# Thirty-two more tokens gathered instead of computed densely in the PEER layer of a two-block transformer kernel

## The chip, the cores and the metric

One core of one Trainium2 chip. The metric is the device time of one execution in microseconds (us); lower is better. All data is float32, the inputs lie in DRAM, and one launch computes both blocks.

## The reference, cut to what matters

The kernel computes `second_block(first_block(x, ...), ...)` for 512 tokens of width 1024. The first block is a mixer (neighbourhood attention and HGRN2) with its projections, and then the PEER layer, which is where the change lies:

```python
PEER_HEADS, PEER_NKEYS, PEER_TOPK, PEER_DQ = 8, 128, 16, 256   # 128 * 128 = 16384 experts
def peer_ffn(h, wq, sub_keys, u, v):
    def block(t):                                   # 128 tokens
        q = (t @ wq).reshape(128, 8, 2, 128)
        s = jnp.einsum('tpcd,pckd->tpck', q, sub_keys)
        s1, i1 = lax.top_k(s[:, :, 0], 16)
        s2, i2 = lax.top_k(s[:, :, 1], 16)
        cand = (s1[..., :, None] + s2[..., None, :]).reshape(128, 8, 256)
        cidx = (i1[..., :, None] * 128 + i2[..., None, :]).reshape(128, 8, 256)
        top, pos = lax.top_k(cand, 16)
        idx = jnp.take_along_axis(cidx, pos, axis=-1)
        g = jax.nn.softmax(top, axis=-1)
        a = jax.nn.gelu(jnp.einsum('tpkd,td->tpk', u[idx], t), approximate=False)
        return jnp.einsum('tpk,tpkd->td', g * a, v[idx])
```

Each token thus has 8 × 16 = 128 chosen experts, each a row of `u` and a row of `v`. In `first_block` it stands as `x = x + gt2 * peer_ffn(modulate(rms_norm(x, norm2), sh2, sc2), ...)`; gt2, and the second block's shift, scale and gate, are products of a vector with `w_mod` and `w_ada`.

## The kernel before

**Numbers.** A product is made of three float32r matmuls: each operand is split into a high part (a cast on ScalarE, line 190) and a low part (the difference, on VectorE, line 191), and high × high, high × low and low × high are added up (`proj_T`, `proj_N`, `s_part`, `v_part`; all matmuls are recorded at line 176). Weights come through one ring of four raw buffers `wr` and four each of `wh` and `wl` (pool "weightsM"), 0.524 MB a load, all issued by SyncE (SP).

**Two ways through PEER.** The 512 tokens are four blocks of 128. Blocks 0 to 2, 384 tokens, are dense. For each of 128 blocks of 128 experts, `s_part` (line 683) multiplies the block's rows of `u` with the 384 tokens (24 matmuls of 384 columns into `pS`) and takes Gelu into a tile `S`. 88 of these (`NSP`) are stored in DRAM (`sd`) and read back later as `Sr`, the others are made in the last stretch. The gates of the dense tokens become a matrix `gd` in DRAM, by products of one-hot tables: for a group of 32 tokens, VectorE compares iotas with the chosen indices (`Rh`, `Lq`), `Lq` is multiplied by the gates (24 of 32 tokens on ScalarE, line 879, 8 on VectorE, line 877), one matmul a token adds up the 128 × 128 table into `pG`, ScalarE copies it into `stg`, and 2 MB go to `gd`. There are 12 groups, and the loop's body stands in lines 860 to 887. In the last stretch (from line 922) `W = S * G` is formed for each expert block, split, and `v_part` multiplies it with the block's rows of `v`: 18 matmuls of 512 columns into the six accumulators `po`.

Block 3 is gathered. One of its tokens sits on each partition, and each of its 128 slots is one indirect DMA, issued by GpSimd (POOL, line 839), of one expert's rows of `u` and `v` for every partition: 1.049 MB into a ring `uv` of four. VectorE forms the dot with the token (line 840, into `pscr`), ScalarE takes Gelu, VectorE multiplies the gate and adds the scaled `v` half to `pacc` (line 846). Two slots make a group; `run_gather` says how many groups are to be done by a point of the program: one in each one-hot group, the other 52 in the last stretch.

**Between them: scores and routing.** Eight steps (line 794) load a piece of `wq`, project all tokens, multiply with the keys and copy the scores of each block into four tables `rsc`. After the steps 1, 3, 5 and 7, `gemv_T` (line 247) computes one modulation vector of `w_mod` or `w_ada` through loads into a ring `wg` of two buffers of its own: eight loads of four small matmuls each (`tp`), a row, and column products with `pick`. Then `routing` (line 725) takes a block at a time: 16 top-16 lists (`top16`, line 715) into `sv` and `si`, 64 candidates a head, a second top-16, the positions turned into key numbers by table spreads (`eq`, `sif`), the softmax, and for dense blocks three transposes into `selT`. Beside it run the parts 3 to 51 (`PRE` is 52). The gather's buffers are allocated after the routing's pool is closed (`eR.close()`).

**What sets the order.** Instructions of one engine run in the order that Tile's scheduler lists, which departs from the order of the program where pools and inputs decide. A tile with `bufs=n` is a ring, in which a writer waits until the reader of n uses ago is done; a pool opened after another's close waits for its users; `tc.issue_after(x)` puts a block's instructions behind x. SP issues all loads and stores but the gathers, in one queue.

Of the kernel before, what the change touches and what calls it, by code (L numbers as in the profile page):

```python
# [124 lines left out]
NS = 10  # L125
NSP = 88
PRE = 52
GEN = 3
GR = 1
LAST = 4  # L130
# [5 lines left out]
def program(tc, a, out, tap=None):  # L136
# [37 lines left out]

    def mm(ps, lhs, rhs, first=True, last=True):
        PE.matmul(ps, lhs, rhs, start=first, stop=last)  # L176
# [70 lines left out]
    def gemv_T(pl, ps_pool, wname, part, v, slot, bias, tag="pm"):  # L247
        row = pl.tile([P, D], F32, name="row", bufs=1)
        for h2 in range(2):
            ps = ps_pool.tile([P, 512], F32, name=tag)  # L250
            for h in range(2):
                hf = 2 * h2 + h
                for k0 in (0, 4):
                    w = pl.tile([P, 4, GW], F32, name="wg", bufs=2)
                    DMA.dma_start(w.rearrange("p k n -> p (k n)"), a[wname][4 * part + hf][:, k0 * GW:(k0 + 4) * GW])
                    gemv_rows(ps[:, h * GW:(h + 1) * GW], w, k0)
            S.copy(row[:, h2 * 512:(h2 + 1) * 512], ps)
        ps = ps_pool.tile([P, 512], F32, name=tag)[:, :2 * KT].rearrange("p (k o) -> p k o", o=2)
        for kt in range(KT):
            mm(ps[:, kt, :], row[:, kt * P:(kt + 1) * P], pick[:, v:v + 2])  # L260
        V.tensor_add(modT[:, slot, :], ps[:, :, 0], bias)
# [353 lines left out]
    nd = ND * P  # L615
# [8 lines left out]
    gd = dp.tile([32, P, ND * 4, P], F32, name="gd")  # L624
    sd = dp.tile([NSP, P, ND * P], F32, name="sd")
    mp = pool(eM, "mid")
    gt2T = modT[:, 5, :]
    h2g = {b: mp.tile([P, D], F32, name=f"h2_{b}") for b in range(ND, NB)}
    idx = {b: mp.tile([P, P], I32, name=f"idx{b}") for b in range(ND, NB)}
    gate = {b: mp.tile([P, P], F32, name=f"gate{b}") for b in range(ND, NB)}  # L630
# [3 lines left out]
    def h2_of(b, x):  # L634
        t = h2g[b] if b in h2g else st.tile([P, D], F32, name="h2t")
        r = rstd_of(x, t)
        V.scalar_tensor_tensor(t, x, r, A2, op0=OP.mult, op1=OP.mult)
        V.tensor_add(t, t, B2)
        c0 = b * P
# [58 lines left out]
    for e in range(EARLY):  # L698
        DMA.dma_start(sd[e], s_part(e, V.tensor_tensor))
    eR = ExitStack()  # L700
# [14 lines left out]
    def top16(src, w, val, pos):  # L715
        t = r2.tile([P, P], F32, name="mr", bufs=2)[:, :w]
# [8 lines left out]
    def routing(b, sc):  # L725
        sv = r2.tile([P, 16, 16], F32, name="sv", bufs=2)
        si = r2.tile([P, 16, 16], U32, name="si", bufs=2)
        for j in range(16):
            top16(sc[:, j, :], P, sv[:, j, :], si[:, j, :])
# [39 lines left out]
        for s_ in range(2):  # L769
            eq = r2.tile([P, 8, 16, 16], BF16, name="eq", bufs=2)  # L770
# [496 lines left out]
```

## Time and profile before

| | |
|---|---|
| median of 3 runs | 2346.18 us (2343.89 to 2346.5) |
| the profiled execution, its own time | 2337.86 us |
| its span in the trace | 2336.1 us, 34601 instructions |
| granted clock of TensorE, mean | 0.992 |
| TensorE matmul (PE) busy | 2259.9 us, 97% |
| weight load (PEld) busy | 1942.3 us, 83% |
| VectorE (DVE) busy | 1598.4 us, 68% |
| ScalarE (ACT) busy | 980.3 us, 42% |
| GpSimd (POOL) busy | 249.1 us, 11% |
| moved by DMA | 481.74 MB, mean 206 GB/s |

The span is what the trace covers of the execution. A busy PE is one with a matmul in its pipeline: their ends are modelled and they overlap, so the distance between two starts, not the duration of one, tells the pace. Waits stand in brackets behind a row, with what ended them. The granted clock is the share of 2.4 GHz that TensorE had; the DMA share is the mean of the core's 16 DMA engines.

### The profile page before, as it was taken

Reading aid. Unit: us, or ns where it says so; the run is one execution under the profiler, and the core shown is the slowest. Engines: PE = TensorE matmul, PEld = TensorE weight load, DVE = VectorE, ACT = ScalarE, POOL = GpSimd, SP = SyncE. Lnnn points to the kernel's source line nnn. Section 1 sums busy time; section 2 is a strip of 40 time slices with the busy share of each in tenths; the row PEclk is TensorE's granted clock in tenths of the full one; section 3 lists DMA queues with packets and bytes.
Section 4 is the critical chain, followed back from the end, with each engine's and each line's share of the span. In section 5 each row is a group of like instructions: output and inputs, shape, how many; then the busy total and the mean of one; then the engine's idle time right before and its main releaser. Section 6 shows DMA issues by size and latency. Waiting matters only on the chain. (4 is left out here: it accounts for less than half of the span.)

```text
span 2336.1 us, 34601 instructions
## 1 busy us (share of the span) xinstructions
PE 2259.9 (97%) x13097; PEld 1942.3 (83%) x13097; DVE 1598.4 (68%) x3193; ACT 980.3 (42%) x1828; POOL 249.1 (11%) x159
## 2 busy tenths in 40 slices
PE   7999999998999999999999999999999999989998
PEld 4899986597779999999988888888888786666888
DVE  3674723354359977999689888888898627767344
ACT  4432333333234335877534333333333434446421
POOL 0000000000000000322222222222130000000000
PEclk9999999999999999999999999999999999999999
DMA  7111135625555574999999999999997231120221
GB/s 265 55 57 55 52 118 178 212 101 178 165 196 158 163 258 153 328 320 319 333 360 396 406 347 349 354 362 363 360 380 263 88 103 42 50 86 28 98 92 55
DMA packets 170871, 481.74 MB, mean 206 GB/s; under 512 B 14864, under 2 KB 87952, under 8 KB 153168
## 3 DMA queue, kind: packets, MB, share of 16 engines
q1 hardware_dynamic: 152272, 345.31, 42.7%
q0 software_dynamic: 18432, 134.23, 14.7%
q8 instruction: 103, 1.69, 0.3%
q14 instruction: 64, 0.52, 0.1%
HBM read 431.76 MB, written 46.66 MB: 205 GB/s over the span
## 5 line engine op out<-in xcount | busy, mean ns | idle before, releaser
L191 DVE TENSOR_TENSOR wl<-wr,wh 128x1024 fp32r<-128x1024 f32 (+1 forms) x378 | 456.7, 1211 | 362.3 <-ACT wh L190 359.8
L190 ACT CAST wh<-wr 128x1024 fp32r<-128x1024 f32 (+1 forms) x378 | 394.0, 1043 | 440.4 <-PE pm L176 196.1
L176 PE MATMUL pS<-h2h,wh 128*128 128x384 f32 x1024 | 348.2, 340 | 7.3 <-ACT S L695 7.2
L176 PE MATMUL pS<-h2h,wl 128*128 128x384 f32 x1024 | 346.1, 338 | 0.0
L176 PE MATMUL pS<-h2l,wh 128*128 128x384 f32 x1024 | 345.5, 337 | 0.0
L839 POOL DMA_INDIRECT uv<-in_uv_dram,idx x128 | 225.8, 1764 | 1006.9 <-DVE pacc L846 688.8
L176 PE MATMUL po<-wl,Wh 128*128 128x512 f32 x768 | 299.6, 390 | 1.8 <-DVE wl L191 1.8
L176 PE MATMUL po<-wh,Wl 128*128 128x512 f32 x768 | 299.5, 390 | 0.0
L176 PE MATMUL po<-wh,Wh 128*128 128x512 f32 x768 | 298.9, 389 | 0.0
L176 PEld LDWEIGHTS pS<-h2h,wh 128*128 128x128 f32 x1024 | 193.4, 189 | 11.7 <-ACT S L695 8.7
L176 PEld LDWEIGHTS pS<-h2l,wh 128*128 128x128 f32 x1024 | 193.3, 189 | 2.0 <-issue 0.8
L176 PEld LDWEIGHTS pS<-h2h,wl 128*128 128x128 f32 x1024 | 193.2, 189 | 0.0
L190 ACT CAST Wh<-W 128x384 fp32r<-128x384 f32 x128 | 65.7, 513 | 267.8 <-PE po L176 162.1
L176 PE MATMUL pm<-h2h,wh 128*128 128x512 f32 x432 | 173.5, 402 | 0.2 <-ACT cr L1106 0.2
L176 PE MATMUL pm<-h2h,wl 128*128 128x512 f32 x432 | 171.8, 398 | 0.0
L176 PE MATMUL pm<-h2l,wh 128*128 128x512 f32 x432 | 171.8, 398 | 0.0
L176 PEld LDWEIGHTS po<-wl,Wh 128*128 128x128 f32 x768 | 144.1, 188 | 31.9 <-DVE wl L191 2.6
L176 PEld LDWEIGHTS po<-wh,Wl 128*128 128x128 f32 x768 | 144.1, 188 | 30.3 <-DVE Wl L191 0.3
L176 PEld LDWEIGHTS po<-wh,Wh 128*128 128x128 f32 x768 | 144.2, 188 | 29.2
L846 DVE SCALAR_TENSOR_TENSOR pacc<-uv,dts,pacc 128x1024 f32<-128x1024 f32 x128 | 163.9, 1281 | 1.9
L840 DVE SCALAR_TENSOR_TENSOR pscr<-uv,h 128x1024 f32<-128x1024 f32 x128 | 156.1, 1219 | 1.9 <-DMA uv<-in_uv_dram,idx 0.9
L191 DVE TENSOR_TENSOR Wl<-W,Wh 128x384 fp32r<-128x384 f32 x128 | 70.8, 553 | 47.9 <-ACT Wh L190 47.8
(410 smaller groups left out, 4100.6 us busy)
## 6 DMA issues: line engine op xcount, KB each, us to landing
wr<-in_uT_dram SPq DMA_DIRECT2D x128, 512.0 KB, 6.0
wr<-in_uv_dram SPq DMA_DIRECT2D x128, 512.0 KB, 7.7
gd<-stg SPq DMA_DIRECT2D x12, 2048.0 KB, 12.6
Gt<-gd SPq DMA_DIRECT2D x32, 768.0 KB, 8.4
sd<-S SPq DMA_DIRECT2D x88, 192.0 KB, 3.9
Sr<-sd SPq DMA_DIRECT2D x88, 192.0 KB, 6.8
wr<-in_w_in_dram SPq DMA_DIRECT2D x32, 512.0 KB, 3.6
wg<-in_w_mod_dram SPq DMA_DIRECT2D x32, 512.0 KB, 4.3
```

Of the source, the lines that this page charges most:

```text
L176: PE.matmul(ps, lhs, rhs, start=first, stop=last)
L190: (ehi or S.copy)(hi, src)
L191: (elo or V.tensor_tensor)(lo, src, hi.bitcast(F32), op=OP.subtract)
L839: G.indirect_dma_start(out=uv, out_offset=None, in_=a["uv"], in_offset=bass.IndirectOffsetOnAxis(ap=idx[b][:, j:j + 1], axis=0))
L840: V.scalar_tensor_tensor(scr, uv[:, :D], 1.0, h2g[b], op0=OP.mult, op1=OP.mult, accum_out=dts[b][:, j:j + 1])
L846: V.scalar_tensor_tensor(acc[b], tl[j - j0][:, D:], dts[b][:, j:j + 1], acc[b], op0=OP.mult, op1=OP.add)
```

## The change

Thirty-two tokens, the last of block 2 (`XB`, rows `r0` = 96 to 127), join the gathered ones.

- They have 128 slots each, and four of a token's slots lie side by side: slot g × 32 + j of the 32 tokens is on partitions 32 g to 32 g + 31, so 32 gathers serve them. The tokens' rows of h2, their indices and gates are copied into that shape by DMAs. At the end two matmuls with `pick` add the four partial sums into rows 96 to 127 of the accumulators of block 2.
- The dense part has `nd` = 352 columns: `s_part` multiplies 352, `sd`, `gd`, `S` and `Sr` shrink, one-hot groups are 11. `W` keeps 384 columns, and GpSimd sets the last 32 to zero, so `v_part` is what it was. `NSP` goes from 88 to 84, `PRE` from 52 to 51, and the `S` ring from 10 to 5.
- Gather buffers and accumulators are laid out ahead of the routing pool. Eight groups (`G0`) of block 3 may run once it is routed, one in each one-hot group, 61 in the last stretch. The dot is written over the `u` half of `uv` (no `pscr`).
- The 16 lists of a block are no longer in `routing`: each score step makes its eight lists (four blocks, two halves) behind its modulation product, from a ring of four score tiles. Blocks are routed in the order 3, 0, 1, 2, and the transposes into `selT` stand behind parts 34, 44 and 50 (`HOLD`).
- The modulation products of the score steps load through the ring `wr`, and their copies and column products are made per half.
- All 32 gate multiplications of a one-hot group, and a spread of `sif` (`sfx`), go to ScalarE.

```diff
-NS = 10
-NSP = 88
-PRE = 52
+NS = 5
+NSP = 84
+PRE = 51
+G0 = 8
+G1 = G0 + 11
+BORDER = (3, 0, 1, 2)
+NLIST = 4
+XG = 32
+HOLD = (34, 44, 50)
...
-    def gemv_T(pl, ps_pool, wname, part, v, slot, bias, tag="pm"):
+    def gemv_T(pl, ps_pool, wname, part, v, slot, bias, tag="pm", share=False):
...
-                    w = pl.tile([P, 4, GW], F32, name="wg", bufs=2)
+                    w = wpool["w"].tile([P, 4, GW], F32, name="wr") if share else pl.tile([P, 4, GW], F32, name="wg", bufs=2)
...
+            for k in range(4):
+                mm(ps[:, k, :], row[:, k * P:(k + 1) * P], pick[:, v:v + 2])
+            V.tensor_add(modT[:, slot, 4 * h2:4 * h2 + 4], ps[:, :, 0], bias[:, 4 * h2:4 * h2 + 4])
...
-    nd = ND * P
+    nd = ND * P - XG
...
+        if b == XB:
+            for g in range(XS):
+                DMA.dma_start(h2g[b][g * XG:(g + 1) * XG, :], t[r0:P, :])
...
+            V.scalar_tensor_tensor(uv[:, :D], uv[:, :D], 1.0, h2g[b], op0=OP.mult, op1=OP.mult, accum_out=dts[b][:, j:j + 1])
...
-    def routing(b, sc):
-        sv = r2.tile([P, 16, 16], F32, name="sv", bufs=2)
-        si = r2.tile([P, 16, 16], U32, name="si", bufs=2)
-        for j in range(16):
-            top16(sc[:, j, :], P, sv[:, j, :], si[:, j, :])
+    def routing(b):
+        sv, si = svs[b], sis[b]
...
-            V.tensor_tensor(eq, eq, sif[:, :, s_, :][:, :, :, None].to_broadcast([P, 8, 16, 16]), op=OP.mult)
+            sfx = r2.tile([P, 8, 16, 16], BF16, name="sfx", bufs=1)
+            S.copy(sfx, sif[:, :, s_, :][:, :, :, None].to_broadcast([P, 8, 16, 16]))
+            V.tensor_tensor(eq, eq, sfx, op=OP.mult)
...
-            for j, t in enumerate((sel[0], sel[1], gt_)):
-                PE.transpose(ps[:, j, :], t, ident)
+            with tc.issue_after(after[HOLD[b]].ins):
+                for j, t in enumerate((sel[0], sel[1], gt_)):
+                    PE.transpose(ps[:, j, :], t, ident)
...
-        for i in range(NB):
+        lists = []
+        for i in BORDER:
...
-            S.copy(scs[i][:, 2 * j:2 * j + 2, :].rearrange("p a b -> p (a b)"), ps[:, :GW])
+            sc = r2.tile([P, 2, P], F32, name="rsc", bufs=NLIST)
+            S.copy(sc.rearrange("p a b -> p (a b)"), ps[:, :GW])
+            lists.append((i, sc))
...
+        for i, sc in lists:
+            for m in range(2):
+                top16(sc[:, m, :], P, svs[i][:, 2 * j + m, :], sis[i][:, 2 * j + m, :])
...
-    for b in reversed(range(NB)):
-        routing(b, scs[b])
+    for b in BORDER:
+        routing(b)
+    run_gather(G0)
     eR.close()
...
-            for tg in range(4):
+            for tg in range(min(4, NTG - 4 * b)):
...
-                    if t8 == 24:
-                        V.tensor_tensor(Lh, Lq, bc(g_), op=OP.mult)
-                    else:
-                        for j in range(8):
-                            S.activation(Lh[:, j, :], Lq[:, j, :], AF.Copy, scale=g_[:, tg * 32 + t8 + j:tg * 32 + t8 + j + 1])
+                    for j in range(8):
+                        S.activation(Lh[:, j, :], Lq[:, j, :], AF.Copy, scale=g_[:, tg * 32 + t8 + j:tg * 32 + t8 + j + 1])
...
-            W = d2.tile([P, nd], F32, name="W")
+            W = d2.tile([P, ND * P], F32, name="W")
+            G.memset(W[:, nd:], 0.0)
...
-                run_gather(GR * ND * 4 - (GR * ND * 4 - len(todo)) * (n + 1) // (P - 10))
+                run_gather(G1 + (len(todo) - G1) * (n + 1) // (P - 10))
...
+            if b == XB:
+                for hf in range(2):
+                    mm(po[b, hf][r0:P, :], pick[:, :XG], acc[b][:, hf * 512:(hf + 1) * 512], False, False)
```

How the instructions stand on three engines, before and with the change. A row is a line of that version's code, the operation, the tiles it writes and reads, the shape, and how many alike follow each other.

TensorE at the first modulation product, behind score step 1: `pm<-h2…` are the score projections, `pm<-keysT` the products with the keys, `tp<-wg` or `tp<-wr` the modulation product and `tp<-pick` its columns. Before:

```order
L176 MATMUL pm<-h2l,wh 128x512
L176 MATMUL tp<-wg,cvec 32x256 x4
L176 MATMUL pm<-h2h,wl 128x512
L176 MATMUL pm<-h2h,wh 128x512
L176 MATMUL pm<-h2l,wh 128x512
L176 MATMUL pm<-h2h,wl 128x512
L176 MATMUL pm<-h2h,wh 128x512
L176 MATMUL tp<-wg,cvec 32x256 x4
L176 MATMUL pm<-h2l,wh 128x512
```

With the change:

```order
L184 MATMUL pm<-keysT,pqT 128x128 x3
L184 MATMUL tp<-wr,cvec 32x256
L184 MATMUL pm<-keysT,pqT 128x128 x5
L184 MATMUL tp<-wr,cvec 32x256 x14
L184 MATMUL tp<-pick,row 128x2 x4
L184 MATMUL tp<-wr,cvec 32x256 x16
L184 MATMUL tp<-pick,row 128x2 x4
L184 MATMUL pm<-h2h,wh 128x512
L184 MATMUL pm<-h2l,wh 128x512
```

The products that stood four at a time between projections stand together ahead of the next step. In SP's queue the loads follow suit: eight of `w_mod` or `w_ada`, then four of `wq`, where they alternated before.

VectorE at the lists behind the same kind of step (`sv`, `si` values and places of a list, `wl` the low part of a weight, `modT` the modulation vector). Before, where all lists stand between the parts:

```order
L720 MAX sv<-mr 128x8
L718 MAX_INDEX si<-sv,rsc_4985 128x8
L721 MAX_INDEX si<-sv,mr 128x8
L718 MAX_INDEX si<-sv,rsc_4985 128x8
L191 TENSOR_TENSOR wl<-wr,wh 128x1024 x2
L717 MAX sv<-rsc_4985 128x8 x2
```

With the change, behind an odd score step:

```order
L772 MATCH_REPLACE mr<-sv_5020,rsc 128x128
L773 MAX sv_5020<-mr 128x8
L774 MAX_INDEX si_5024<-sv_5020,mr 128x8
L269 TENSOR_TENSOR modT<-tp,vecs 128x4
L199 TENSOR_TENSOR wl<-wr,wh 128x1024 x4
L770 MAX sv_5021<-rsc 128x8 x2
L771 MAX_INDEX si_5025<-sv_5021,rsc 128x8
L772 MATCH_REPLACE mr<-sv_5021,rsc 128x128
```

Lists now stand among the score steps, and the four splits of the next step's weights have lists ahead of them and behind them, with the sum of the modulation product between.

GpSimd from the routing to the last stretch. Before:

```order
L708 IOTA ior_4976 128x128
L839 DMA uv<-in_uv_dram,idx_4186 128x2048 x128
```

With the change:

```order
L761 IOTA ior_5011 128x128
L736 DMA uv<-in_uv_dram,idx_4196 128x2048 x42
L970 MEMSET W 128x32 x4
L736 DMA uv<-in_uv_dram,idx_4196 128x2048
L970 MEMSET W 128x32
L736 DMA uv<-in_uv_dram,idx_4196 128x2048
```

The memsets of W's last columns stand in the queue of the gathers, one for each expert block.

## Rows read from the trace of the kernel before

**Rows 1.** Stretches: us; busy PE PEld DVE ACT POOL (count); clock, DMA share, GB/s.

```profile
543.00:680.00 137.00, 133.56 (x803) 101.19 (x802) 46.41 (x177) 41.09 (x72) 0.00 (x0) 1.00 0.52 170
680.00:917.00 237.00, 232.36 (x1353) 227.17 (x1351) 203.31 (x841) 91.82 (x128) 5.48 (x4) 0.99 0.59 191
917.00:1186.00 269.00, 263.91 (x1762) 259.52 (x1763) 237.73 (x253) 200.38 (x484) 72.74 (x28) 1.00 0.91 314
1186.00:1765.00 579.00, 577.20 (x2713) 497.95 (x2713) 507.91 (x700) 212.52 (x330) 147.54 (x96) 1.00 0.96 369
1765.00:1840.00 75.00, 75.00 (x333) 62.05 (x332) 55.07 (x79) 27.93 (x41) 1.43 (x2) 1.00 0.52 178
```

**Rows 2.** Timeline of TensorE, neighbouring matmuls: start us, duration us, instruction.

```profile
850.16 0.33 PE L176 MATMUL pS<-h2h,wl 128*128 128x384 f32 x1
850.33 0.33 PE L176 MATMUL pS<-h2h,wh 128*128 128x384 f32 x1
...
1400.68 0.39 PE L176 MATMUL po<-wh,Wl 128*128 128x512 f32 x1
1400.91 0.39 PE L176 MATMUL po<-wh,Wh 128*128 128x512 f32 x1
...
117.81 0.28 PE L176 MATMUL pm<-wl,hTh 128*128 128x256 f32 x1
...
118.89 0.28 PE L176 MATMUL pm<-wl,hTh 128*128 128x256 f32 x1
```

**Rows 3.** Timeline of TensorE, one-hot products (a float32 matmul is two records).

```profile
973.38 3.73 PE L176 MATMUL pG<-Rh,Lq 128*128 128x128 f32 x32
```

**Rows 4.** Timeline of TensorE, a modulation product among the scores.

```profile
578.22 0.64 PE L176 MATMUL tp<-wg,cvec 128*32 128x256 f32 x8 [0.83 <-DMA wg<-in_w_mod_dram]
578.79 0.50 PE L176 MATMUL pm<-h2h,wl 128*128 128x512 f32 x1
...
590.42 1.84 PE L176 MATMUL tp<-pick,row 128*128 128x2 f32 x16
592.12 0.47 PE L176 MATMUL pm<-h2h,wh 128*128 128x512 f32 x1
```

**Rows 5.** The page's costliest groups: busy us, mean ns | idle before, releaser.

```profile
L191 DVE TENSOR_TENSOR wl<-wr,wh 128x1024 fp32r<-128x1024 f32 (+1 forms) x378 | 456.7, 1211 | 362.3 <-ACT wh L190 359.8
L190 ACT CAST wh<-wr 128x1024 fp32r<-128x1024 f32 (+1 forms) x378 | 394.0, 1043 | 440.4 <-PE pm L176 196.1
L176 PE MATMUL pS<-h2h,wh 128*128 128x384 f32 x1024 | 348.2, 340 | 7.3 <-ACT S L695 7.2
...
L176 PEld LDWEIGHTS pS<-h2h,wh 128*128 128x128 f32 x1024 | 193.4, 189 | 11.7 <-ACT S L695 8.7
...
L846 DVE SCALAR_TENSOR_TENSOR pacc<-uv,dts,pacc 128x1024 f32<-128x1024 f32 x128 | 163.9, 1281 | 1.9
L840 DVE SCALAR_TENSOR_TENSOR pscr<-uv,h 128x1024 f32<-128x1024 f32 x128 | 156.1, 1219 | 1.9 <-DMA uv<-in_uv_dram,idx 0.9
```

**Rows 6.** Tile wg from 545 to 690 us.

```profile
DMA to landing us min/median/max: 3.1/4.4/6.3
```

**Rows 7.** Two stretches within the last, columns as in rows 1.

```profile
1226.00:1343.00 117.00, 116.66 (x558) 101.73 (x557) 106.77 (x147) 45.44 (x70) 32.13 (x21) 1.00 1.01 400
1343.00:1693.00 350.00, 350.00 (x1661) 303.80 (x1660) 302.34 (x415) 128.15 (x200) 84.39 (x56) 1.00 0.94 356
```

**Rows 8.** A pause of TensorE and what followed, columns as in rows 1.

```profile
790.00:795.00 5.00, 1.70 (x10) 1.38 (x9) 5.00 (x31) 3.50 (x5) 0.00 (x0) 1.00 0.48 157
...
796.00:799.00 3.00, 3.00 (x11) 3.00 (x11) 3.00 (x13) 0.00 (x0) 0.00 (x0) 0.50 0.24 22
```

**Rows 9.** Timeline of VectorE, one list from its start to the next's.

```profile
814.79 0.07 DVE L718 MATCH_VALUE_LOAD si<-sv,rsc 128x8 f32 x1
...
815.96 0.07 DVE L718 MATCH_VALUE_LOAD si<-sv,rsc 128x8 f32 x1
```

**Rows 10.** Lines of ScalarE from 925 to 1165 us: busy us, mean ns.

```profile
L879 ACT ACTIVATE Lq<-Lq,selT 128x128 f32<-128x128 f32 x267 | 82.2, 392 | 5.1 <-DVE Lq L874 5.1
```

More of the change, by code (lines that the diff above doesn't have):

```diff
@@ L173, in program @@
     DMA.dma_start(vecs, a["vecs"])
+    last_mm = [None]
     def mm(ps, lhs, rhs, first=True, last=True):
-        PE.matmul(ps, lhs, rhs, start=first, stop=last)
+        last_mm[0] = PE.matmul(ps, lhs, rhs, start=first, stop=last)
     class Split:
@@ L699, in program, with gather, run_gather @@
         DMA.dma_start(sd[e], s_part(e, V.tensor_tensor))
+    ug = pool(eM, "uvg", 1)
+    nfB = ug.tile([P, D], F32, name="nfB")
+    DMA.dma_start(nfB, a["rows"][0:1, :].to_broadcast([P, D]))
+    S.activation(nfB, nfB, AF.Square)
+    gt2 = ug.tile([P, D], F32, name="gt2")
+    acc = {b: ug.tile([P, D], F32, name=f"pacc{b}") for b in range(ND, NB)}
+    eU = ExitStack()
+    up = pool(eU, "uv", 4)
+    ux = pool(eU, "uvx", 1)
+    acc[XB] = ux.tile([P, D], F32, name="paccx")
+    dts = {b: ux.tile([P, n], F32, name=f"dts{b}") for b, n in ncol.items()}
+    for b in acc:
+        V.memset(acc[b], 0.0)
+    GRP = 2
+    def gather(b, j0):
+        tl = []
+        for j in range(j0, j0 + GRP):
+            uv = up.tile([P, 2 * D], F32, name="uv")
+            G.indirect_dma_start(out=uv, out_offset=None, in_=a["uv"], in_offset=bass.IndirectOffsetOnAxis(ap=idx[b][:, j:j + 1], axis=0))
+            V.scalar_tensor_tensor(uv[:, :D], uv[:, :D], 1.0, h2g[b], op0=OP.mult, op1=OP.mult, accum_out=dts[b][:, j:j + 1])
+            tl.append(uv)
+        ds_ = dts[b][:, j0:j0 + GRP]
+        S.activation(ds_, ds_, AF.Gelu)
+        V.tensor_mul(ds_, ds_, gate[b][:, j0:j0 + GRP])
+        for j in range(j0, j0 + GRP):
+            V.scalar_tensor_tensor(acc[b], tl[j - j0][:, D:], dts[b][:, j:j + 1], acc[b], op0=OP.mult, op1=OP.add)
+    todo = [(b, j0) for b, n in ncol.items() for j0 in range(0, n, GRP)]
+    prog = [0]
+    def run_gather(upto):
+        for k in range(prog[0], min(upto, len(todo))):
+            gather(*todo[k])
+        prog[0] = max(prog[0], upto)
     eR = ExitStack()
@@ L783, in routing @@
         V.reciprocal(ts_, ts_)
-        gt_ = gate[b] if b in gate else r2.tile([P, P], F32, name="gt_")
+        gt_ = gate[b] if b >= ND else r2.tile([P, P], F32, name="gt_", bufs=2)
         V.tensor_tensor(gt_.rearrange("p (h k) -> p h k", k=16), tm, ts_[:, :, None].to_broadcast([P, 8, 16]), op=OP.mult)
-        if b in idx:
+        if b == XB:
+            xf = r2.tile([P, P], F32, name="xf")
+            xi = r2.tile([P, P], I32, name="xi")
+            V.scalar_tensor_tensor(xf[r0:P], sel[0][r0:P], 128.0, sel[1][r0:P], op0=OP.mult, op1=OP.add)
+            V.tensor_copy(xi[r0:P], xf[r0:P])
+            for g in range(XS):
+                DMA.dma_start(idx[b][g * XG:(g + 1) * XG, :], xi[r0:P, g * XG:(g + 1) * XG])
+                DMA.dma_start(gate[b][g * XG:(g + 1) * XG, :], gt_[r0:P, g * XG:(g + 1) * XG])
+        if b >= ND:
             V.scalar_tensor_tensor(sel[0], sel[0], 128.0, sel[1], op0=OP.mult, op1=OP.add)
@@ L848, in program @@
-    todo = [(b, j0) for b in range(ND, NB) for j0 in range(0, P, GRP)]
-    prog = [0]
-    def run_gather(upto):
-        for k in range(prog[0], min(upto, len(todo))):
-            gather(*todo[k])
-        prog[0] = max(prog[0], upto)
     with ExitStack() as es:
```

78 lines of the change are left out of this document (30 added, 48 removed).

## The prediction

> **What bounds the kernel now.** I read the stretches first [rows 1]: they are cut at the first score projection (543 us), the last score (680), the first one-hot product (917), the first product with V (1186), the last gather (1765) and the last product with V (1840). TensorE is busy 97 to 100% of every one, so it sets the end. A busy TensorE need not be at its pace, so next the start-to-start distances [rows 2]: 173 ns for 384 columns, 227 for 512, 120 for 256 (1.08 us for nine). That is 0.418 ns a column plus 13 ns, at 2.4 GHz (the granted clock is 0.99 to 1.00). One expert block's U product ("part": 24 matmuls of 384 columns) therefore takes 4.15 us, one block's V product (18 of 512) 4.09 us. Against these sums, how much of a stretch is lost? 543 to 680: eight score steps of 48 × 0.227 + 16 × 0.114 = 12.7 us [rows 2, 3] and four modulation products of 8 × 0.57 + 1.70 = 6.3 us [rows 4] make 127 of 137 us. 680 to 917: 55 parts, 228 of 237. 917 to 1186: 41.5 parts and 768 one-hot records of 0.114 us make 260 of 269. 1186 to 1840: 28.5 parts, 128 V blocks and the gt2 spread make 644 of 654. So nearly all is matmul time, and only fewer columns, or fewer stalls, shorten it. What may stop such a saving is in the DMA column [rows 1]: 0.91 and 0.96 of 16 engines busy in the third and fourth stretch.
>
> **The change part by part.**
>
> *Narrower U products.* 128 × 24 = 3072 matmuls (a third of them are the 1024 of [rows 5]) go from 384 to 352 columns: 32 × 0.418 = 13.4 ns each, **-41.1 us**, all on the engine that bounds. The V products keep 512 columns and their number.
>
> *One group of one-hots fewer.* 32 matmuls, 64 records at 0.114 us [rows 3]: **-7.3 us**.
>
> *Modulation products out of the weight ring.* Before, they had their own two buffers and stood between score matmuls. Now their eight loads use the four buffers of the weights, and the order shows them in a clump. I follow one clump from t = 0, the end of an odd step's scores. The first four loads are in: products until 2.2. Their buffers' next loads leave at 0.6, 1.2, 1.7 and 2.3. The first lands a median 4.4 us later [rows 6], the others behind it at about 1.3 us (0.524 MB at the 400 GB/s of rows 7): 5.0 to 8.9, the last product ends at 9.5, and copy and column products at 11. Behind them in SP's queue stand the next step's weights, which need the fifth and sixth buffer: issued at 5.6, landed at about 10.2, cast by 11.3 (1.04 us), split by VectorE (1.2 us) [rows 5] at 12.5. Only then can TensorE's third matmul run. So 12.5 us where 6.3 are work: 6.2 of stall, four times, 25 us; less the 10 lost there now, and 1 to 2 us because the first split behind the last clump stands behind routing instructions: **+16 us**. Queued behind the wait: on TensorE all scores, on VectorE the four splits (behind the modulation's add). Bounds: 0 (the loads run ahead as now) to +28 (each landing the slowest, 6.3 us).
>
> *The clock.* TensorE did 1.7 us of work in 790 to 795, and then had 0.50, which is 1.2 GHz, in 796 to 799 [rows 8]. A clump does some 4 us of work in the 10 us from 2.2 on, so I expect a dip at each. Three us at half pace behind the restart cost 1.5: **+6 us**, bounds 0 and +14.
>
> *Lists behind the scores.* 64 lists at 1.17 us [rows 9]. Eight of them take 9.4 us: those of an even step run under the 12.7 us of the next, those of an odd one are done before the weights above are split. Cost 0; if the clump got shorter than 9.4 us, they would be what is late next. Taking 75 us of VectorE work out of 680 to 917 (203 busy of 237) makes room for 16 gathers (2.35 us each beside the others) and should halve the 9 us lost there: **-4 us**, bounds -9 and +5.
>
> *Gates on ScalarE, one-hot stretch.* The 32 gate multiplications of a group, 24 now, cost 0.31 us each [rows 10]: 2.5 us more on ScalarE, 1.2 less on VectorE. A group then holds 18.8 us of TensorE (3 × 3.84 + 64 × 0.114), some 19 of ScalarE (200 busy in 269 now, which is 15 of 20 for a group with all its copies, less overlap, plus 2.5: 17.5 to 19.3), and 6.3 MB, 18.3 us at 314/0.91 = 345 GB/s. Three engines level lose more to each other than one bound: **+4 us** over 11 groups, bounds 0 and +15. The two table spreads a block (ScalarE copies) run where ScalarE is busy 92 of 237 us: 0.
>
> *The last stretch.* Nine parts move into it (39 instead of 30). To the last gather it has 118 V blocks (482 us) and 36 parts of 3.84 (138): 620 us of TensorE. In that time it moves 118 V blocks and 36 U blocks at 0.524 MB, 122 gathers at 1.049 (61 groups; now 104), 77 S of 0.18, 29.5 G of 0.72: 244 MB, which is 393 GB/s, where 369 are moved now at 0.96 busy. VectorE: 508 of 579 now; 26 gathers and 8 splits more make some 580 of 620, not the bound. DMA is level with TensorE. For 117 us it did 400 GB/s with TensorE 99.7% busy [rows 7], so I take **+10 us**; bounds 0 and +41 (the mean rate of the stretch). The Trainium skill speaks against it: "DMA: Bandwidth & Descriptors", Specifications, gives an HBM limit of about 358 GB/s a core and a derate of 368. By the latter 244 MB would take 663 us, 43 more than TensorE's; rows 7 exceed it for 117 us, so I don't take it for the sum.
>
> *POOL.* The memsets of W's last 32 columns queue behind gathers that wait for a buffer. No row has such a wait: 0 where the casts' lead of several VectorE instructions covers it, at most a gather's issue (147.54 us for 96 in the fourth stretch [rows 1], 1.5 each) in an iteration; inside the bounds above. The 32-row copies of h2, indices and gates: SP has time; 0. The correction's two matmuls, and the second row copy of the three earlier modulation products: **+1 us**.
>
> Sum: -41.1 - 7.3 + 16 + 6 - 4 + 4 + 10 + 1 = **-15 us**. The profiled execution took 2337.9 us, 8.3 below the median 2346.2; I take the difference from the median: **2331 us**. A measurement of this kernel tells about 0.2%, 4.7 us.
>
> **Rivals.**
>
> *DMA becomes the bound of the last stretch: slower.* Place: 1186 to the last gather. If the engines give no more than the stretch's mean of 369 GB/s, it lasts 661 us: +41 where I have +10, sum +16, 2362 us. The gain is gone below 244/(620 + 25) = 378 GB/s. For it: 0.96 busy, and 356 GB/s at 0.94 over 350 us [rows 7], though TensorE lost nothing there. Against: the 400 GB/s. By the 368 of the Trainium skill's section above it would come to 2364. Chance 0.20.
>
> *The clumps cost nothing.* If loads lead as they do now, the 16 and 6 go and the sum is -37: 2309 us. For it: SP's queue is nearly empty there (0.52 busy). Against: the ring has four buffers, and a clump needs ten. Chance 0.15.
>
> *Clumps dearer, one-hot stretch level.* +28 and +14 in place of 16 and 6, and +10 at the groups: 2357 at the worst, about 2346 at half of it, no change. Chance 0.14.
>
> *The columns save nothing.* A weight load shows 189 ns [rows 5], longer than the 173 between starts, and loads are busy all through. If they set the pace, the 41 us are lost: 2372. Against: 256 columns, with the same loads, start every 120 ns. Chance 0.04.
>
> **How the numbers follow.** The forecast has 0.47, nearly all of it faster. Faster: 0.44 + 0.15 + a little of the third rival = 0.60; same: 0.15, from the third rival and the forecast's edge; slower: 0.20 + 0.04 + 0.01 = 0.25. Range 2304 to 2362: it holds the forecast with the bounds of single terms, the second rival, the third, and the first up to its own price; the loads' case and a DMA worse than that lie outside. The forecast's own range is 2315 to 2342.
>
> **What would show it.** U matmuls 160 ns apart; four idle stretches of 4 to 8 us between 550 and 700 whose releaser is a load of wr, dips of the clock at them, and the first routing part 15 to 20 us later than 680; groups of 19 to 19.5 us; first V product at about 1125 to 1135; the stretch from there to the last V product 690 to 700 us with DMA at 0.98. Wrong: loads of wr or uv as the main releasers of TensorE or VectorE in that stretch (first rival), or no idle time at the clumps (second).

## The result and the profile after

The change takes 2367.04 us (median of 6 runs, 2365.09 to 2372.22) where the kernel before takes 2346.34 (6 runs): ratio 1.0094, 95% interval 1.0076 to 1.0113. It is 20.7 us slower. The prediction said 2331 and a range up to 2362, so both the time and the sign were missed.

The profiled execution took 2367.62 us. The page's first lines:

```profile
span 2365.8 us, 34863 instructions
...
PE 2250.0 (95%) x13037; PEld 1915.8 (81%) x13037; DVE 1644.6 (70%) x3295; ACT 1001.0 (42%) x1908; POOL 314.1 (13%) x319
```

The stretches, cut at the same events, with the columns of [rows 1]:

```profile
547.00:695.00 148.00, 134.69 (x734) 101.32 (x733) 88.86 (x470) 34.53 (x65) 0.00 (x0) 0.88 0.37 129
695.00:931.00 236.00, 217.33 (x1342) 209.63 (x1340) 195.00 (x607) 107.81 (x150) 31.12 (x20) 0.96 0.74 267
931.00:1160.00 229.00, 216.70 (x1518) 212.77 (x1517) 190.00 (x199) 196.07 (x515) 45.70 (x24) 0.98 0.91 312
1160.00:1795.00 635.00, 619.59 (x2935) 530.41 (x2935) 564.11 (x792) 224.88 (x360) 211.09 (x233) 0.99 0.96 374
1795.00:1866.00 71.00, 70.90 (x329) 58.73 (x327) 54.53 (x80) 27.98 (x41) 4.41 (x14) 1.00 0.50 178
```

TensorE's work did shrink. Two neighbouring U products on its timeline start 160 ns apart, where [rows 2] has 173:

```profile
781.19 0.32 PE L184 MATMUL pS<-h2h,wh 128*128 128x352 f32 x1
781.35 0.32 PE L184 MATMUL pS<-h2l,wh 128*128 128x352 f32 x1
```

So a part costs 3.84 us for 4.15, as forecast, and with the one-hot group the matmuls need some 47 us less. Everything else is time that TensorE now loses. For each stretch I compare its length with what its matmuls need at their own pace (parts, V blocks of 4.09 us, one-hot records of 0.114 us). "Scores" runs from the first copy of the projected queries to the last product with the keys, "routing" from there to the first copy of a one-hot product, "last" from the first to the last product with V; what stands between is the one-hot stretch:

| stretch, us | before | needs | lost | change | needs | lost |
|---|---|---|---|---|---|---|
| ahead of the scores | 553.3 | | | 547.5 | | |
| scores | 127.1 | | | 147.6 | | |
| routing | 238.5 | 229 | 9 | 235.6 | 206 | 30 |
| one-hot groups, first S tiles | 267.4 | 258 | 10 | 228.9 | 211 | 18 |
| last | 653.7 | 653 | 1 | 706.3 | 679 | 27 |
| behind | 496.0 | | | 500.0 | | |

The scores grew by 20.5 us with the same matmuls but for 16 small ones that now stand in the routing, and the routing, the one-hot stretch and the last one lose 55 us more than before. By the records in the trace these three need 44 us less. With 5.8 us less ahead and 3.9 more behind, that is 29.6 us; the two executions differ by 29.8. The medians differ by less, because the execution profiled of the kernel before lay 8 us under its median. I therefore take the size of a cause from timed runs, and its place from the traces.

### The profile page after: what moved, and what is told of

It reads as the page before. It is cut to its first block, busy times and chain, and to the rows that moved or that the text cites. A ratio compares the mean times of both kernels' runs of the same rounds, so it can differ in the third digit from the quotient of the medians.

```text
span 2365.8 us, 34863 instructions
## 1 busy us (share of the span) xinstructions
PE 2250.0 (95%) x13037; PEld 1915.8 (81%) x13037; DVE 1644.6 (70%) x3295; ACT 1001.0 (42%) x1908; POOL 314.1 (13%) x319
## 5 line engine op out<-in xcount | busy, mean ns | idle before, releaser
L736 POOL DMA_INDIRECT uv<-in_uv_dram,idx x160 | 274.2, 1714 | 841.9 <-DVE pacc L743 501.6
L184 PE MATMUL pS<-h2h,wh 128*128 128x352 f32 x1024 | 338.8, 331 | 13.0 <-ACT S L712 13.0
L184 PE MATMUL pS<-h2h,wl 128*128 128x352 f32 x1024 | 336.8, 329 | 3.9 <-DVE wl L199 3.7
L184 PE MATMUL pS<-h2l,wh 128*128 128x352 f32 x1024 | 335.6, 328 | 0.0
L737 DVE SCALAR_TENSOR_TENSOR uv<-uv,h 128x1024 f32<-128x1024 f32 x160 | 192.7, 1219 | 24.2 <-DMA uv<-in_uv_dram,idx 23.8
L740 ACT ACTIVATE dts<-dts 128x2 f32<-128x2 f32 x80 | 16.3, 204 | 259.4 <-DVE uv L737 259.4
L913 ACT ACTIVATE Lq<-Lq,selT 128x128 f32<-128x128 f32 x352 | 109.4, 394 | 4.6 <-DVE Lq L911 4.6
```

The lines of the kernel that those rows point to most:

```text
L184: last_mm[0] = PE.matmul(ps, lhs, rhs, start=first, stop=last)
L736: G.indirect_dma_start(out=uv, out_offset=None, in_=a["uv"], in_offset=bass.IndirectOffsetOnAxis(ap=idx[b][:, j:j + 1], axis=0))
L737: V.scalar_tensor_tensor(uv[:, :D], uv[:, :D], 1.0, h2g[b], op0=OP.mult, op1=OP.mult, accum_out=dts[b][:, j:j + 1])
L740: S.activation(ds_, ds_, AF.Gelu)
L913: S.activation(Lh[:, j, :], Lq[:, j, :], AF.Copy, scale=g_[:, tg * 32 + t8 + j:tg * 32 + t8 + j + 1])
```

## The experiments

Lengths of stretches are cut as in the table above, ratios are to the kernel before. Four of the results side by side, the others in the text:

| run | median us | ratio | interval |
|---|---|---|---|
| own_buffers | 2340.51 | 0.9987 | 0.9972 to 1.0002 |
| no_extra_gathers | 2342.56 | 0.9997 | 0.9983 to 1.0011 |
| odd_half_rows | 2339.09 | 0.9984 | 0.9963 to 1.0005 |
| own_spread_ten | 2318.20 | 0.9882 | 0.9854 to 0.9910 |

### own_buffers: the modulation products out of the shared ring

```diff
-                    w = wpool["w"].tile([P, 4, GW], F32, name="wr") if share else ...
+                    w = up.tile([P, 2 * D], F32, name="uv")[:, :4 * GW].rearrange("p (k n) -> p k n", n=GW) if share else ...
```

> The change, but the modulation products of the score steps load into the four gather buffers, which are idle then, and not into the ring of the weights. In the change the scores take 147.6 us from the first projection to the last product with the keys (before: 127.1), with four clumps of modulation products, pauses of some 5 us and 10 to 14 us at half clock at each. Theory A, the shared ring is the cause: the scores go back to 125 to 132 us, the four low-clock stretches between 570 and 720 us go, and the time falls by 20 to 30 us, to 2337 to 2347. Rival, the lists or the score tiles (a ring of four) hold the scores back: the stretch stays above 140 us and the time at 2360 or more.

The ratio falls from 1.0094 to 0.9987, some 25 us. The scores take 125.9 us and the routing 229.6, 21.7 and 6.0 less (the fourth clump stands at the routing's start). Theory A holds. In the change, TensorE's timeline at the first clump reads:

```profile
571.40 1.05 PE L184 MATMUL tp<-pick,row 128*128 128x2 f32 x8 [0.69 <-ACT row L265]
573.38 0.64 PE L184 MATMUL tp<-wr,cvec 128*32 128x256 f32 x8 [0.93 <-DVE sv L773]
574.57 0.64 PE L184 MATMUL tp<-wr,cvec 128*32 128x256 f32 x8 [0.55 <-DMA wr<-in_w_mod_dram]
576.85 1.08 PE L184 MATMUL tp<-wr,cvec 128*32 128x256 f32 x8 [1.64 <-DMA wr<-in_w_mod_dram]
578.10 1.08 PE L184 MATMUL tp<-wr,cvec 128*32 128x256 f32 x8 [0.17 <-DMA wr<-in_w_mod_dram]
579.94 1.86 PE L184 MATMUL tp<-pick,row 128*128 128x2 f32 x8 [0.76 <-ACT row L265]
581.67 0.77 PE L184 MATMUL pm<-h2h,wh 128*128 128x512 f32 x1
582.24 0.63 PE L184 MATMUL pm<-h2l,wh 128*128 128x512 f32 x1
582.67 0.63 PE L184 MATMUL pm<-h2h,wh 128*128 128x512 f32 x1
```

The pauses in brackets add up to 4.7 us, most of them for a load of `wr` or for the row's copy. The clock adds to them: behind the clump 512 columns are 0.43 us apart, not 0.227. The stretches around it, columns as in [rows 1]:

```profile
565.00:576.00 11.00, 8.04 (x76) 5.13 (x75) 7.75 (x52) 2.47 (x6) 0.00 (x0) 0.98 0.48 166
576.00:586.00 10.00, 8.22 (x35) 5.51 (x36) 7.51 (x23) 4.57 (x5) 0.00 (x0) 0.51 0.80 278
586.00:596.00 10.00, 10.00 (x48) 7.96 (x46) 0.85 (x1) 1.17 (x2) 0.00 (x0) 1.00 0.51 170
```

The granted clock is 1.2 GHz for 10 us. It is so at each of the four clumps, for 10.2, 10.2, 13.7 and 13.7 us; [rows 8] had shown about 3. Part of these times TensorE stands idle, so by estimate (half of the rest) each costs 4 to 6 us: the four clumps lose 20 us in pauses and some 18 by the clock, about as much. In own_buffers no low clock falls inside the scores, whose row reads:

```profile
554.00:680.00 126.00, 122.68 (x755) 92.86 (x754) 93.36 (x474) 38.57 (x69) 0.00 (x0) 1.00 0.56 182
```

VectorE does the lists there as in the change (93 us of work), at no cost.

### before_shared_ring: that part alone

```diff
-        gemv_T(rb, tp, "w_mod", 5, 0, 5, bmT[:, 40:48], "tp")
+        gemv_T(rb, tp, "w_mod", 5, 0, 5, bmT[:, 40:48], "tp", True)
...
-            gemv_T(rb, tp, "w_ada", part, 2, 6 + part, baT[:, part * 8:part * 8 + 8], "tp")
+            gemv_T(rb, tp, "w_ada", part, 2, 6 + part, baT[:, part * 8:part * 8 + 8], "tp", True)
```

> The kernel before with one part of the change alone: the modulation products of the score steps load into the ring of the weights. Theory, the shared ring makes the clumps: the scores go from 127 us to 140 to 150, low-clock stretches of 10 us and more show at the modulation products, and the time rises by 18 to 28 us, ratio 1.008 to 1.012. Rival, it needs the lists behind the scores too (they delay the column products' add on VectorE): under 10 us.

Ratio 1.0162 (1.0116 to 1.0208): 38 us, even more than forecast. The scores take 154.6 us and the routing 253.3, together 42 more than before, and the clock is at half for 13.7 us at each of the first three products. The row of the scores, which had 1.00 in the clock's column before:

```profile
571.00:726.00 155.00, 138.29 (x743) 104.35 (x745) 38.27 (x173) 35.04 (x66) 0.00 (x0) 0.87 0.36 123
```

The lists aren't needed for it. Its profiled execution shows 18 us more ahead of the scores as well, where the edit changes nothing that I can name. TensorE is at half clock there for 51 us in its trace and for 17 in that of the kernel before, and half of the difference is 17 us, which by estimate is the 18; why the clock was low more often stays open.

### no_extra_gathers: the price of the 32 gathers

```diff
-    todo = [(b, j0) for b, n in ncol.items() for j0 in range(0, n, GRP)]
+    todo = [(b, j0) for b, n in ncol.items() if b != XB for j0 in range(0, n, GRP)]
```

> The change without its 32 extra gathers (the 32 tokens get no PEER output; the routing, copies and narrower products stay). In the change the stretch from the first to the last product with V is 706 us for 676 us of matmuls, DMA 0.97 busy at 374 GB/s. Theory A, the last stretch is bound by DMA with the extra 33.6 MB (90 us at 374 GB/s, of which TensorE's own work covers most): it falls to 676 to 684 us and the time by 20 to 30 us, to 2337 to 2347. Rival, the narrower stages lose their time for other reasons (GpSimd's memsets, the shorter S ring): it stays above 695 us, and the time at 2355 or more.

The ratio falls to 0.9997, 23 us, and the last stretch from 706.3 to 681.0 us, with 679 needed. Its row up to the last gather shows a TensorE that never waits:

```profile
1156.00:1743.00 587.00, 586.50 (x2832) 508.60 (x2832) 486.40 (x669) 216.66 (x336) 148.41 (x196) 1.00 0.91 342
```

So the two causes, clumps and extra gathers, are worth 25 and 23 us. Together they are what the columns and the one-hot group saved; that they add up wasn't tried in one run. The change is 21 us slower all the same, so some 20 us more are lost elsewhere, by the table in the routing and the one-hot stretch.

### What in the gathers costs: half_bytes, odd_half_rows, odd_no_sum, zero_once

The waits of the last stretch (engine, what waits, for what; us, times, longest) name more than one engine. Before:

```profile
POOL uv L839 <- DVE pacc L846: 415.5, 63, 17.3
ACT Wh L190 <- PE po L176: 157.9, 67, 3.3
ACT dts L843 <- DVE pscr L840: 65.2, 26, 7.0
...
ACT wh L190 <- DMA wr<-in_uv_dram: 11.8, 9, 3.5
```

The change:

```profile
POOL uv L736 <- DVE pacc L743: 214.2, 64, 8.4
ACT dts L740 <- DVE uv L737: 212.1, 55, 9.3
POOL W L970 <- DVE Wl L199: 112.4, 47, 9.4
ACT wh L198 <- DMA wr<-in_uv_dram: 87.6, 43, 7.2
```

ScalarE, which used to wait for TensorE, now waits for loads of V and for the dots. In both kernels GpSimd waits for VectorE's sum before it can issue the next gather, since the sum frees the buffer. Four runs separate bytes, VectorE and GpSimd.

half_bytes fetches half rows for the 32 extra gathers:

```diff
-            G.indirect_dma_start(out=uv, out_offset=None, in_=a["uv"], ...
+            G.indirect_dma_start(out=uv if b != XB else uv[:, :D], out_offset=None, in_=a["uv"] if b != XB else a["uv"].rearrange("n (t d) -> (n t) d", d=D), ...
...
```

> The change with the 32 extra gathers fetching half a row, 4 KB a partition in place of 8, and the sum taken from that half (the 32 tokens' PEER output is not the reference's). GpSimd issues as many gathers, VectorE and ScalarE do the same work on them; only 16.8 MB of transfers go. Theory DMA: what the extra gathers cost in the last stretch (706 us against 681 without them) is their bytes; at 374 GB/s half of them are 45 us of the DMA engines, more than the 25 lost, so the stretch falls to 680 to 690 us and the time by 15 to 25 us, to 2342 to 2352. Rival, engines' order (ScalarE behind the dots, VectorE 0.89 busy, GpSimd's longer queue): the stretch stays above 700 and the time at 2360 or more.

Ratio 1.0090 (1.0067 to 1.0114), last stretch 701.8 us: by the letter the rival's numbers. But the edit was badly placed. The extra gathers are the last in the list, so only the last quarter moved fewer bytes. Its windows (columns as in [rows 1]) show the loss ahead of that point and none behind it:

```profile
1170.00:1570.00 400.00, 384.39 (x1828) 326.74 (x1828) 351.71 (x499) 138.58 (x224) 135.77 (x147) 1.00 0.96 370
...
1650.00:1791.00 141.00, 141.00 (x680) 122.06 (x679) 134.19 (x188) 54.20 (x86) 47.71 (x55) 1.00 0.87 297
```

odd_half_rows therefore does it to every second gather of the whole list:

```diff
+            half = j % 2 == 1
-            G.indirect_dma_start(out=uv, out_offset=None, in_=a["uv"], ...
+            G.indirect_dma_start(out=uv[:, :D] if half else uv, out_offset=None, in_=a["uv"].rearrange("n (t d) -> (n t) d", d=D) if half else a["uv"], ...
...
```

> The change with every second gather (80 of 160, over the whole last stretch, not the last quarter alone as in half_bytes) fetching half a row, and the sum taken from that half (wrong output). The count of gathers and the work of every engine stay; 42 MB of transfers go, some 32 MB of them in the last stretch. Theory DMA: the last stretch, 706 us for 679 of matmuls, falls to 679 to 684 us, and the time by 22 to 35 us, to 2332 to 2345. Rival, VectorE and ScalarE waiting on each other in order: it stays above 697 us and the time above 2355.

The last stretch takes 679.0 us, its matmuls' own time, with VectorE as busy as in the change:

```profile
1162.00:1762.00 600.00, 600.00 (x2898) 521.14 (x2899) 563.27 (x792) 224.95 (x359) 218.97 (x232) 1.00 0.94 345
```

odd_no_sum keeps the bytes and leaves out every second weighted sum:

```diff
-        for j in range(j0, j0 + GRP):
+        for j in range(j0, j0 + GRP, 2):
             V.scalar_tensor_tensor(acc[b], tl[j - j0][:, D:], ...
```

> The change with the weighted sum left out for every second gathered slot (wrong output): 80 VectorE instructions of 1.28 us fewer, 61 of them (78 us) in the last stretch, and their buffers come free after the dot. The bytes stay. Theory DMA: the last stretch stays at 695 to 708 us. Rival, VectorE (0.89 busy there) or the return of the buffers holds the stretch: it falls to 679 to 688 us. The routing has 8 such sums fewer: 4 to 8 us less in either case. Time 2350 to 2362 by the first, 2330 to 2345 by the second.

The ratio is 1.0062 (1.0035 to 1.0089). The last stretch, 688.2 us, lies in neither theory's range, nearer the rival's; the time, 2356.92, lies in the first one's. So neither is right alone. Its row is the surprise:

```profile
1165.00:1771.00 606.00, 599.78 (x2882) 518.78 (x2883) 498.91 (x730) 223.50 (x359) 160.89 (x231) 0.99 0.99 390
```

The same transfers went through at 390 GB/s. So 374 isn't all that the DMA engines give. My reading is that with four buffers, each held until VectorE has formed its sum, they are not asked for more; no run has more buffers, and the edit takes work from VectorE as well as freeing buffers sooner, so these two aren't told apart. The pace that the change needs is 374 × 635 us over the 608 that remain without the loss, 390 GB/s. I read the two runs together so: that pace is out of reach while the buffers return late, and nearly within reach when they don't. Fewer bytes recover all of the 27 us, fewer sums two thirds. (The routing took 237.4 us; the 4 to 8 us that I expected there didn't come.)

zero_once takes the memsets out of GpSimd's queue:

```diff
+        Ws = [d2.tile([P, ND * P], F32, name=f"W{i}", bufs=1) for i in range(2)]
+        for W in Ws:
+            G.memset(W[:, nd:], 0.0)
...
-            W = d2.tile([P, ND * P], F32, name="W")
-            G.memset(W[:, nd:], 0.0)
+            W = Ws[n % 2]
```

> The change with two fixed W tiles whose last 32 columns GpSimd sets to zero once, in place of a memset for each expert block. In the change GpSimd's memsets waited 150 us in the last stretch for a free W, with gathers queued behind them. Theory DMA: the memsets cost nothing, since a gather that leaves later finds the DMA engines just as full: the last stretch stays at 700 to 710 us and the time within 4 us of the change's, 2363 to 2371. Rival, the memsets hold the gathers back: the stretch falls to 690 or less and the time by 10 us or more.

Ratio 1.0114 (1.0085 to 1.0142), last stretch 701.5 us. GpSimd's 112 us of waiting for W cost nothing that can be told.

### Where the gathers stand: own_early, own_late, own_spread

Every run whose name begins with own_ has the edit of own_buffers too, which the diffs don't repeat; own_early also has both table spreads on VectorE.

```diff
-NSP = 84
-PRE = 51
+NSP = 96
+PRE = 63
...
-G0 = 8
+G0 = 22
...
```

> The change with four edits: the modulation products load into the idle gather buffers; both table spreads stay on VectorE; 12 U products of the last stretch stand in the routing (63 ahead of the one-hot groups, 96 stored); 22 groups of gathers in place of 8 are issued ahead of the one-hot groups. The columns saved are the same. The last stretch then moves by estimate 216 to 224 MB in 628 us of TensorE's work, 345 to 357 GB/s, under the 374 at which it lost time. Theory DMA and clumps: the last stretch loses under 8 us against its matmuls (it takes 628 to 640 us), the scores take 126, and the time falls below before's, to 2312 to 2328, ratio 0.986 to 0.994. Rival, the routing stretch has no room for 14 more groups on VectorE or ScalarE (2.4 us a gather on an engine that is 0.82 busy): TensorE loses 20 to 35 us more there, and the time is 2335 to 2350.

2360.68 us, ratio 1.0085 (1.0059 to 1.0112): the rival's way, and over its range by 11 us. The last stretch is freed, 634.4 us for 633 of matmuls at 364 GB/s, but the routing takes 310.1 us for 257, and the one-hot stretch loses 19 us more than in own_buffers. That the added parts and gathers only move the loss is what the run shows; its four edits aren't separated.

```diff
-G0 = 8
+G0 = 0
```

> The change with the modulation products in the gather buffers and no group of gathers ahead of the one-hot groups (0 for 8): 16 gathers, 16.8 MB, move into the last stretch. Beside own_buffers (routing 230 us, last stretch 708, 2340 us). Theory DMA: at 374 GB/s they add 45 us to a stretch that is full, so it takes 745 to 755 us, the routing gives back 5 to 12 us (its early gathers hold ScalarE and VectorE), and the time is 2370 to 2385. Rival, the last stretch isn't bound by bytes: it grows by under 15 us, and the time stays at 2335 to 2352.

2388.45 us, ratio 1.0199 (1.0178 to 1.0219), a little over the range. The last stretch takes 759.8 us, 52 more than in own_buffers for 16 gathers, 3.2 us each. Its row up to the last gather:

```profile
1116.00:1804.00 688.00, 638.23 (x2937) 536.30 (x2938) 599.51 (x849) 226.02 (x368) 252.61 (x248) 0.97 0.96 369
```

With more bytes to move, the engines moved them no faster than in the change, and below the 390 of odd_no_sum. The routing, with no gather's arithmetic in it, takes 213.1 us and loses 7. Taken together, own_late, own_buffers and own_early make a line: 0, 16 and 44 early gathers lose 7, 24 and 53 us in the routing, some 1.05 us for each. own_early has other edits there too, so this is no more than an indication.

own_spread moves nothing between stretches, it only lets the gathers of the last one run on for six blocks more:

```diff
-                run_gather(G1 + (len(todo) - G1) * (n + 1) // (P - 10))
+                run_gather(G1 + (len(todo) - G1) * (n + 1) // (P - 4))
```

> The change with the modulation products in the gather buffers, and the gathers of the last stretch spread over 124 expert blocks in place of 118. In the change the DMA engines are 0.97 busy until the last gather and 0.50 busy in the 70 us behind it. Theory DMA: a pace 5% lower, 370 MB/ms on the mean of the whole stretch, is near what they move (374), so most of the loss goes: last stretch 685 to 697 us where own_buffers has 708, time 2322 to 2334. Rival: the late sums now stand ahead of the last products and uncover 5 to 10 us at the end, or the loss isn't the pace: 2338 to 2348.

2328.15 us, ratio 0.9930 (0.9903 to 0.9956). The last stretch falls from 708.1 to 693.7 us: the DMA engines were half idle behind the last gather (0.50 in the change's last row above), and that time is now used.

### Smaller parts: ten_s_tiles, gates_spread_back, own_spread_ten

```diff
...
+    s5 = pool(eU, "sbuf5", 5)
+    ring = lambda e: sbuf if (e - NSP) % 10 < 5 else s5
-    for _ in range(NS):
+    for _ in range(10):
         e = fresh.pop(0)
-        Ss[e] = s_part(e)
+        Ss[e] = s_part(e, None, ring(e))
...
```

> The change with ten S tiles ahead of the last stretch in place of five (five more in the space that the one-hot stage leaves). Theory: the five parts fewer uncover the trip of the last group through DRAM (7.0 us of pause at 1152 us, behind it 6.8 us at half clock): the pause falls to under 3 us and the time by 5 to 9 us, to 2358 to 2362. Rival: the parts are only moved, the DMA of the last stretch sets its end, which comes no sooner with 5 loads less in it or the pause covered: 2364 to 2369. If S tiles also give the last stretch more lead: 2350.

2360.83 us, ratio 1.0080 (1.0050 to 1.0110). The median fits, the interval takes in the change's own ratio. The trace shows one pause of 2.6 us there in place of the 7.0 us ahead of the first V product.

```diff
-            sfx = r2.tile([P, 8, 16, 16], BF16, name="sfx", bufs=1)
-            S.copy(sfx, sif[:, :, s_, :][:, :, :, None].to_broadcast([P, 8, 16, 16]))
-            V.tensor_tensor(eq, eq, sfx, op=OP.mult)
+            V.tensor_tensor(eq, eq, sif[:, :, s_, :][:, :, :, None].to_broadcast([P, 8, 16, 16]), op=OP.mult)
...
-                    for j in range(8):
+                    if t8 == 24:
+                        V.tensor_tensor(Lh, Lq, bc(g_), op=OP.mult)
+                    for j in range(8 if t8 < 24 else 0):
```

> The change with a quarter of the gate multiplications and both table spreads back on VectorE, as before. In the change the one-hot groups lose 8 us more against their matmuls than before, and ScalarE waits 15 us for the spreads in the routing, with TensorE behind it. Theory A, ScalarE is the wrong place: the time falls by 6 to 14 us, to 2353 to 2361. Rival, VectorE is as full there (191 busy of 230 us): 2365 to 2375.

Ratio 1.0109 (1.0078 to 1.0139): no gain, the rival. Routing and one-hot stretch are 3.0 and 3.6 us shorter in its trace, too little to show in the times.

own_spread_ten is own_spread with the ten S tiles and the spreads on VectorE:

> own_spread, with both table spreads back on VectorE and ten S tiles ahead of the last stretch. Theory: ten S tiles cover the trip of the last one-hot group (4 to 8 us) and the spreads no longer hold ScalarE in the routing (3 us): 2312 to 2326, ratio 0.987 to 0.993, the fastest so far. Rival: these are within the noise of own_spread: the same time within 4 us.

Its ratio of 0.9882 is 28 us under the kernel before, the fastest of all; its interval lies under own_spread's median. The last stretch:

```profile
1156.00:1784.00 628.00, 628.00 (x2955) 531.86 (x2954) 565.15 (x788) 229.81 (x363) 195.30 (x233) 1.00 0.98 377
1784.00:1829.00 45.00, 45.00 (x191) 34.80 (x189) 39.55 (x61) 17.06 (x25) 6.04 (x8) 1.00 0.50 179
```

TensorE has no pause up to the end. With the loads (own_buffers), the pace (own_spread) and the cover of the last group (ten S tiles) put right, 28 of the some 47 us saved are kept.

### The early gathers: own_early_no_gelu, own_early_dma_only

ScalarE's timeline in own_buffers shows how a gather in the routing may hold TensorE. ScalarE runs in order, the Gelu of a part stands behind these, and TensorE's next part behind that Gelu:

```profile
800.32 0.20 ACT L740 ACTIVATE dts<-dts 128x2 f32<-128x2 f32 x1 [4.75 <-DVE uv L737]
...
838.26 1.90 ACT L826 COPY sfx<-sif 128x2048 bf16<-128x2048 bf16 x1 [7.74 <-DVE eq L827]
```

```diff
+        if prog[0] >= G0:
             S.activation(ds_, ds_, AF.Gelu)
```

> The change with the modulation products in the gather buffers, and the Gelu of the eight early groups left out (wrong output): ScalarE no longer stands waiting for the dots of those groups, VectorE and the transfers do the same. own_buffers' routing took 229.6 us, own_late's (no early group) 213.1. Theory A, ScalarE's order holds TensorE (it waited 20 us for the dots and 24 for the spreads' tables there): the routing falls to 215 to 222 us. Rival, VectorE is simply full while it routes: 226 to 231 us.

The routing takes 224.3 us, between both ranges: 5.3 of the 16.5 us over own_late. The time is 2333.55, ratio 0.9955 (0.9931 to 0.9978). But own_spread, whose code differs from own_buffers' in the last stretch alone, has a routing of 225.7 us in its trace, so two traces of one routing differ by 3.9. The 5.3 are hardly more than that, and the intervals of this ratio and of own_buffers' overlap.

```diff
+            if prog[0] < G0:
+                continue
             V.scalar_tensor_tensor(uv[:, :D], uv[:, :D], 1.0, h2g[b], ...
...
+        if prog[0] < G0:
+            return
         ds_ = dts[b][:, j0:j0 + GRP]
```

> As own_early_no_gelu, with the dots and sums of the eight early groups left out too (wrong output): the 16 gathers are only transfers. Theory A or VectorE: 212 to 216 us, as without early groups. Rival, the transfers delay the loads of U's rows: 222 us or more.

233.1 us (time 2345.53, ratio 0.9991, 0.9968 to 1.0014): the transfers alone cost as much as the whole gathers. The run took the pace away with the work, though. Nothing held the buffers, the gathers went off back to back, and loads of U came late. Of ScalarE's waits in the routing the row on them reads:

```profile
ACT wh L198 <- DMA wr<-in_uT_dram: 34.2, 9, 7.5
```

The window of the burst, columns as in [rows 1]:

```profile
760.00:800.00 40.00, 30.33 (x155) 28.88 (x153) 27.56 (x118) 15.01 (x17) 10.64 (x9) 0.87 1.02 421
```

own_buffers has no such wait among its large ones. So the early gathers cost 13 to 17 us in the routing (own_late against own_spread and own_buffers). ScalarE's order is not shown to be a large part of it, and how the loss divides between that, VectorE, the spreads' tables and the transfers stays open.

## Why the prediction was wrong

**Right.** The columns and the one-hot group saved what was said. The clumps were forecast at 22 us (16 and 6), and own_buffers takes out 25 in time, 27.7 in the stretches. ScalarE's gates and the memsets cost little or nothing.

**The clock term.** Its sum hid two errors that cancel in part. The pauses are shorter than worked out, 20 us over the four clumps for 25; the half clock is longer. I took three us behind a restart from [rows 8], 1.5 us lost each, 6 in all. It lasted 10 to 14 us, some 18 lost in all. (own_buffers keeps about 8 us of both at these places, so about 30 of the 38 go with its edit; its stretches show 27.7.) What [rows 8] shows is a single pause with full work behind it; a clump is a series of pauses among small matmuls. Which of these makes the difference wasn't tried.

**The last stretch, +10, was +26.** This is the largest loss, and the step that failed is "so I take +10 us" from the 400 GB/s of [rows 7]. I had worked out the need, 393 GB/s, and the mean of 369. A best piece of 117 us isn't what this kernel's full stretch sustains: the change got 374. The reading of this stretch before was off as well: "644 of 654" counted 28.5 parts where the trace has 30, so it had next to nothing to lose (1 us in the table), not 10. The first rival was the right mechanism with too high a price, +41. By the Trainium skill, "DMA: Bandwidth & Descriptors", Specifications, the derate of 368 gave 43. The runs moved 374 to 390, so they contradict it as a limit, though the direction that it gave was the right one. What neither rival nor sum had is the share of VectorE, whose fewer sums alone brought 18 of the 27 us back (odd_no_sum).

**The routing, -4, was +15.** This is the second step that failed, and its miss is as large: 19 us, or 15 by own_spread's trace. "Makes room for 16 gathers ... and should halve the 9 us lost there" treated VectorE's free time as a pool. Without early gathers the loss is 7 us (own_late), near what I said; the 16 early gathers then add 13 to 17. Which engine's wait carries that stays open.

**The one-hot stretch, +4, was +8.** The 7.0 us pause ahead of the first V product was missing: the diff showed the S ring going from 10 to 5, and I gave it no term, though these parts cover the last group's trip through DRAM.

**Chances.** Slower had 0.25, 0.20 of it for the first rival alone. Its chance was too low with 0.96 of the engines busy in the profile, and the clumps, the routing and the last stretch were treated as if one miss excluded the others. All three came on the dear side.

## What to carry to other kernels

A saving on the engine that bounds is kept only if the other queues can feed it at the new pace: divide the bytes of a stretch by its new length, and where that is over the rate which the same stretch sustains now as a whole, take the sustained rate, not its best piece. Loads that join another load's ring inherit its order, and the pauses they made here cost about as much again in TensorE's clock; a buffer that is idle at the time was a better place for them. Transfers that are spread to the end of a stretch, with cover for the hand-over between stages, brought more (25 us between own_buffers and own_spread_ten by their ratios) than moving them to a stage that seemed to have room.

## What the runs showed of the hardware

- The transfers of one core went at 374 GB/s over 635 us in the change, where TensorE lost time, at 377 over 628 us in own_spread_ten, where it lost none, and at 390 over 606 us, engines 0.99 busy, where half of the sums were gone (odd_no_sum); a burst of gathers of 8 KB rows beside U's loads had 421 over 40 us. The Trainium skill, "DMA: Bandwidth & Descriptors", Measured, has 425 for 16 MB from a core whose neighbour is idle; the burst agrees with it, the mixed stretch of this kernel stays below.
- At each clump of the change the granted clock stayed at 0.50 for 10 to 14 us (0.51 on the mean of 576 to 586), though no pause of TensorE at the first was over 1.64 us; the one pause of [rows 8] was followed by some 3.
- The same program's last 500 us, which no edit touched, took 495 to 497 or 499 to 500 us from profile to profile, with one half-clock stretch of 10 to 14 us more in the longer.
